# An inverse and a solve whose matmuls go over more columns than are used

## The chip, the cores and the metric

The kernel runs on one core of a Trainium2 chip. The metric is the device time of one execution in microseconds: 1938.36 us before the change, the median of three runs from 1925.35 to 1941.91.

## The reference, cut to what matters

One inference step of a two-layer recurrent decoder trunk, for a prompt of 528 tokens (16 meta tokens and 512) and 32 sample tokens (8 sequences of 4), width 1024. Layer 0 mixes with gated linear attention (GLA) and an RWKV-7 recurrence side by side; layer 1 mixes with gated DeltaNet (GDN). Each mixer is followed by a convolutional feed-forward part. The change touches what stands for the two recurrences. For GDN the reference has it openly, chunk by chunk:

```python
a_mat = jnp.where(strict, jnp.einsum('bhlk,bhmk->bhlm', ki, ki) * dec, 0.0) * bi[..., :, None] + eye
rhs = jnp.concatenate([vi * bi[..., None], ki * (bi * jnp.exp(gam))[..., None]], axis=-1)
sol = lax.linalg.triangular_solve(a_mat, rhs, left_side=True, lower=True, unit_diagonal=True)
```

RWKV-7 is a scan over tokens in the reference (`s = s * w + (s a) b + v k`); the kernel brings it into the same form, a unit triangular system for each tile of tokens.

## The kernel before, in words

**Tiles.** The 560 tokens stand in five tiles of 112, 112, 112, 96 and 128 (`TILES`; the last has 96 prompt and 32 sample tokens). A "row" count of 112, 96 or 128 below is the length L of such a tile. Heads are taken four at a time: RWKV has two groups of four heads, GDN too. So each of the two recurrences has 2 x 5 tiles, and for every one of them `prep` builds four triangular matrices, calls `tri_inverse` (L708 on) and then `tri_solve` (L769 on), and `step` carries the state on. `core(g)` (L1117 for RWKV, L1774 for GDN) calls `prep(i)` ahead of `step(i-1)`, so one tile's inverse stands beside the state step of the tile before.

**The inverse.** `tri_inverse` doubles block inverses in fp16: T starts as the transpose of the inverse of 2x2 blocks, W as that inverse itself. At level q, with blocks of b = 2, 4, ... 64 columns, four matmuls (one for each head) make `px` = a x T (L737), VectorE masks it into `X` (L738), four make `pt` (L747) and four `pw` (L753), and VectorE adds them to T (L758) and W (L765). Every second block of b columns holds what is new, so `px` and `pt` go over those columns alone (`up`, which is `upper(ap, b, L)`): 56, 48 or 64 of 112, and so on. `pw` goes over all L columns. `X` is set to zero by GpSimd (L734) before VectorE writes the new blocks. The last level (b = 64) has no `pt`. So an inverse has six `px`, five `pt` and six `pw`, each of four matmuls.

**The solve.** `tri_solve` works in fp32r with one refinement step: p0 = W r, p1 = (three terms with x0: identity, `ah`, `al`), p2 = W times the residual. `prod` (L777) issues, for each head i, one matmul a term over the `kd` right sides of that head (`kd` x `w` columns). For RWKV w is 64, for GDN 128; kd is 2, except in a group's first tile, where it is 1. So RWKV's matmuls have 128 columns (64 in the first tile) and GDN's 256 (128 in the first tile).

**What runs beside it, and the order.** While a group's tiles are worked on, a generator issues the projections of later work (`k.beside`, `k.tick`): matmuls at L148, three for each product because fp32 is split into high and low parts. RWKV's first group has them all the way, its second group has GLA's own loop (L1250 to L1330: `pr`, `pv`, `pa`, `po`, `pS`) beside it instead; GDN's groups have GDN's projections and gates, and the norm of the first group (L201, L217). The order of each engine's instructions is set when the program is built: the framework plans it from priorities and its own costs of instructions, and each engine then works strictly in that order.

Of the kernel before, what the change touches and what calls it, by code (L numbers as in the profile page):

```python
# [688 lines left out]
def upper(ap, b, L):  # L689

    m = pairs(b, L)
    if m == 1:
        return ap[..., 0:b]
    return ap[..., 0 : 2 * b * m].rearrange("... (k c) -> ... k c" if len(ap.shape) == 2 else "p n (k c) -> p n k c", c=2 * b)[..., 0:b]


def lower(ap, b, L):

    full = L // (2 * b)
    out = []  # L700
    if full:
        out.append(ap[:, :, 0 : full * 2 * b].rearrange("p n (k c) -> p n k c", c=2 * b)[:, :, :, b : 2 * b])
    if L - full * 2 * b > b:
        out.append(ap[:, :, full * 2 * b + b : L])
    return out


def tri_inverse(k, pool, pp, tag, lv, a, Wr, L, n):  # L708

    nc = k.nc
    two = lambda name: pool.tile([128, 2, n, 128], F16, tag="so" + tag, name=name, bufs=2)
    ps = lambda name: pp.tile([128, n, 128], F32, tag="mx" + tag, name=name)
    bc = lambda ap: ap.unsqueeze(1).to_broadcast([L, n] + list(ap.shape[1:]))
    ta, wx = two("ta"), two("wx")
    T, a16, W = ta[:, 0], ta[:, 1], wx[:, 0]
    Xs = [pool.tile([128, n, 128], F16, tag="X" + tag, name="X"), wx[:, 1]]
    nc.scalar.copy(a16[:L, :, :L], a[:L, :, :L])  # L720
    nc.vector.tensor_mul(W[:L, :, :L], a[:L, :, :L], bc(lv[:L, 0, :L]))
    nc.vector.tensor_add(W[:L, :, :L], W[:L, :, :L], bc(k.ident16[:L, :L]))
    p0 = ps("p0")
    for i in range(n):
        nc.tensor.matmul(p0[:L, i, :L], W[:L, i, :L], k.ident16[:L, :L], start=True, stop=True)
    nc.scalar.copy(T[:L, :, :L], p0[:L, :, :L])
    for q in range(1, 7):
        b = 1 << q
        if b >= L:
            break  # L730
        k.tick()
        up = lambda ap: upper(ap, b, L)
        X = Xs[q % 2]
        nc.gpsimd.memset(X, 0.0)  # L734
        px = ps("px")
        for i in range(n):
            nc.tensor.matmul(up(px[:L, i]), a16[:L, i, :L], up(T[:L, i]), start=True, stop=True)  # L737
        nc.vector.tensor_tensor(up(X[:L]), up(px[:L]), bc(up(lv[:L, q])), op=ALU.mult)  # L738
        last = 2 * b >= L
        k.tick()  # L740
        if not last:
            pt = ps("pt")
            ta = cfg("TA", 0) and (n == 4 or cfg("TB", 1))
            for i in range(n):
                if ta:
                    nc.tensor.matmul(up(pt[:L, i]), k.ident16[:L, :L], up(T[:L, i]), start=True, stop=False)
                nc.tensor.matmul(up(pt[:L, i]), W[:L, i, :L], up(X[:L, i]), start=not ta, stop=True)  # L747
        pw = ps("pw")
        wa = False and not last
        for i in range(n):  # L750
            if wa:
                nc.tensor.matmul(pw[:L, i, :L], k.ident16[:L, :L], W[:L, i, :L], start=True, stop=False)
            nc.tensor.matmul(pw[:L, i, :L], X[:L, i, :L], W[:L, i, :L], start=not wa, stop=True)  # L753
        if not last:
            if ta:
                nc.scalar.copy(up(T[:L]), up(pt[:L]))
            else:
                nc.vector.tensor_add(up(T[:L]), up(pt[:L]), up(T[:L]))  # L758
        else:
            nc.scalar.copy(Wr[:L, :, 0:b], W[:L, :, 0:b])  # L760
        for p, v, w in zip(*(lower(x[:L], b, L) for x in (pw, Wr if last else W, W))):
            if wa:
                nc.scalar.copy(v, p)
            else:
                nc.vector.tensor_add(v, p, w)  # L765
    return Wr


def tri_solve(k, pool, pp, tag, sub, W, ah, al, idr, R, L):  # L769


    nc = k.nc
    _, kd, n, w = R.shape
    m = min(n, 512 // (kd * w))
    tl = lambda name: pool.tile([128, kd, m, w], F32R, tag="so" + tag, name=name, bufs=2)

    def prod(name, terms):  # L777
        t = pp.tile([128, m, kd, w], F32, tag="mx" + tag, name=name)
        for i in range(m):
            for j, (a, x) in enumerate(terms):  # L780
                nc.tensor.matmul(t[:L, i], a(h0 + i), x[:L, :, i], start=(j == 0), stop=(j == len(terms) - 1))  # L781
        return t[:L].rearrange("p n k v -> p k n v")

    h = lambda a: lambda i: a[:L, i, :L]
    for h0 in range(0, n, m):
        r = R[:L, :, h0 : h0 + m]
        rr = tl("sol_r")
        nc.scalar.copy(rr[:L], r)
        p0 = prod("p0", [(h(W), rr)])
        k.tick()  # L790
        x0 = tl("sol_x")
        nc.scalar.copy(x0[:L], p0)
        p1 = prod("p1", [(lambda i: idr[:L, :L], x0), (h(ah), x0), (h(al), x0)])
        k.tick()
        rr2 = tl("sol_r")
        (nc.vector.tensor_sub if sub else nc.vector.tensor_add)(rr2[:L], r, p1)
        if cfg("RA", 0) and sub:
            p2 = prod("p2", [(lambda i: idr[:L, :L], x0), (h(W), rr2)])
            nc.scalar.copy(r, p2)
        else:  # L800
            p2 = prod("p2", [(h(W), rr2)])
            nc.vector.tensor_add(r, p2, x0.bitcast(F32)[:L])


class RWKV:
# [113 lines left out]
    def prep(self, prs, i):  # L919
# [38 lines left out]
        if ty and cfg("RS", 0) == 1:  # L958
            self.sr = self.read_states(prs)
        W = tri_inverse(k, self.pc, self.mx, par, self.lv, ma[:, 0], P("Wr", [128, 4, 128], F32R), L, 4)  # L960
        pv = bank([128, 4, 64], "pv")
        for h in range(4):
# [425 lines left out]
class GDN:  # L1388
# [195 lines left out]
    def prep(self, g, kq, i):  # L1584
# [56 lines left out]
        if ty and cfg("GS", 1):  # L1641
            sr = self.read_states(g, ks, Gr, R, bank)
        W = tri_inverse(k, self.p1, self.mx, par, self.lv, A, P("Wr", [128, 4, 128], F32R), L, 4)
        if ty and not cfg("GS", 1):
            sr = self.read_states(g, ks, Gr, R, bank)
# [251 lines left out]
def trunk(tc, a, o):  # L1897
# [7 lines left out]
    y=(128, KT, NT), shift=(128, KT, 9), gla_p=(2, 128, 128), gla_s=(2, 128, 8, 128), rwkv_p=(4, 128, 64),  # L1905
# [35 lines left out]
```

## Time and profile before

| | before |
| --- | --- |
| median of three runs | 1938.36 us (1925.35 to 1941.91) |
| profiled execution: time | 1941.04 us |
| profiled execution: span from first to last instruction | 1939.1 us |
| TensorE matmul busy | 1820.7 us, 94% |
| VectorE, ScalarE, GpSimd busy | 1169.9, 751.6, 437.9 us |
| mean granted TensorE clock | 0.949 of full speed |

In the rows, PE is TensorE's matmuls, DVE is VectorE, ACT ScalarE, POOL GpSimd. A matmul's form is written as rows of the moving operand * output rows, then rows x columns. Matmuls are pipelined, so a single one lasts some 0.2 to 0.4 us by its own, while the next starts much earlier; what a stream of them costs is seen from start to start. Where several equal ones follow each other, the timeline shows them as one row with a count, from the first start to the last end. PEclk is the granted TensorE clock: 1.00 is 2.4 GHz and 0.50 is 1.2 GHz. RWKV's groups lie at about 80 to 290 us and 260 to 480 us, GDN's at about 1100 to 1270 us and 1270 to 1420 us; the feed-forward parts lie behind each.

### The profile page before, as it was taken

The page shows a single profiled execution, that of the slowest core. Times are in us where ns is not written, and L with a number is a line of the kernel's source. Part 1 is how long each engine was busy: PE and PEld are TensorE (multiplying, and loading weights), DVE is VectorE, ACT ScalarE, POOL GpSimd, SP SyncE. Part 2 cuts the span into 40 slices and gives each one's busy share as a digit, 9 for nine tenths or more (in the row PEclk, how much of TensorE's full clock was granted, in tenths as well). Part 3 has the DMA queues.
Part 4 walks back from the last instruction along what each step waited for, and adds up shares of the span by engine and source line. Part 5 has one row for each costly group of instructions (what it writes and reads, how often), then busy time and mean ns, then how long its engine had stood idle before and what let it go on. Part 6 is the DMA issues. An engine that isn't in the chain of part 4 may idle for free.

```text
span 1939.1 us, 34294 instructions
## 1 busy us (share of the span) xinstructions
PE 1820.7 (94%) x13877; PEld 1694.1 (87%) x13877; DVE 1169.9 (60%) x2085; ACT 751.6 (39%) x1396; POOL 437.9 (23%) x705
## 2 busy tenths in 40 slices
PE   8998899899989999999979999899989999999996
PEld 8897788676889999999968997788679899999995
DVE  5766434446786535535776787687578653453466
ACT  6563323344353223213455454444244432232233
POOL 1323334212241000000141343332236200000001
PEclk9999999669899999999988999999789999999998
DMA  5110122301412222222322212412233122222231
GB/s 205 51 38 23 57 82 82 97 19 38 158 37 79 86 88 88 87 84 85 101 70 61 77 37 63 145 65 74 64 119 108 38 87 88 88 88 88 88 92 47
DMA packets 67358, 153.64 MB, mean 79 GB/s; under 512 B 15656, under 2 KB 26728, under 8 KB 67200
## 3 DMA queue, kind: packets, MB, share of 16 engines
q1 hardware_dynamic: 62784, 142.68, 23.9%
q10 hardware_dynamic: 3104, 4.15, 0.7%
q0 software_dynamic: 1312, 4.63, 0.6%
q8 instruction: 109, 1.79, 0.4%
q14 instruction: 49, 0.40, 0.1%
HBM read 136.72 MB, written 14.70 MB: 78 GB/s over the span
## 4 chain that ended last, share of the span: by engine, by line
PE 58%; DVE 9%; DMA 2%; issue 2%; ACT 2%; POOL 1%; POOLq 0%; SPq 0%; ACTq 0%; DVEq 0%
PE pd L148 13%; PE pg L148 13%; PE pu L148 13%; PE ph L148 7%; PE lead L148 2%; PE p L781 1%; DVE r L511 1%; DVE r L564 1%; DVE r L563 1%; PE psr L272 1%; PE pn L201 1%; PE pst L544 1%; PE pS L1701 1%; PE pw L753 1%; PE pm L1625 1%
## 5 line engine op out<-in xcount | busy, mean ns | idle before, releaser
L95 ACT CAST wh<-wraw 128x1024 fp32r<-128x1024 f32 x179 | 187.4, 1047 | 471.3 <-issue 163.2
L96 DVE TENSOR_TENSOR wl<-wraw,wh 128x1024 fp32r<-128x1024 f32 x158 | 193.9, 1227 | 205.9 <-ACT wh L95 205.9
L148 PE MATMUL ph<-xh,wh 128*128 128x280 f32 (+3 forms) x928 | 287.9, 311 | 16.1 <-ACT cp L1510 7.8
L148 PE MATMUL ph<-xh,wl 128*128 128x280 f32 (+3 forms) x928 | 285.8, 308 | 0.0
L148 PE MATMUL ph<-xl,wh 128*128 128x280 f32 (+3 forms) x928 | 285.7, 308 | 0.0
L148 PEld LDWEIGHTS ph<-xh,wh 128*128 128x128 f32 x928 | 181.1, 195 | 25.0 <-ACT cp L1510 8.0
L148 PE MATMUL pg<-xh,wl 128*128 128x264 f32 (+3 forms) x640 | 186.7, 292 | 0.0
L148 PE MATMUL pu<-xh,wl 128*128 128x264 f32 (+3 forms) x640 | 186.7, 292 | 0.0
L148 PE MATMUL pg<-xh,wh 128*128 128x264 f32 (+3 forms) x640 | 186.0, 291 | 0.0
L148 PE MATMUL pu<-xh,wh 128*128 128x264 f32 (+3 forms) x640 | 185.9, 291 | 0.0
L148 PE MATMUL pu<-xl,wh 128*128 128x264 f32 (+3 forms) x640 | 185.7, 290 | 0.0
L148 PE MATMUL pg<-xl,wh 128*128 128x264 f32 (+3 forms) x640 | 185.7, 290 | 0.0
L148 PEld LDWEIGHTS ph<-xh,wl 128*128 128x128 f32 x928 | 180.9, 195 | 5.2 <-issue 3.7
L148 PEld LDWEIGHTS ph<-xl,wh 128*128 128x128 f32 x928 | 181.1, 195 | 4.5 <-issue 3.1
L380 POOL COPY cn<-gp 128x2 f32<-128x2 f32 x44 | 31.3, 712 | 573.2 <-ACT gp L378 573.2
L148 PE MATMUL pd<-hl,wh 128*128 128x280 f32 (+1 forms) x512 | 148.8, 291 | 0.1
L148 PE MATMUL pd<-hh,wl 128*128 128x280 f32 (+1 forms) x512 | 148.7, 291 | 0.0
L148 PE MATMUL pd<-hh,wh 128*128 128x280 f32 (+1 forms) x512 | 147.8, 290 | 0.0
L148 PEld LDWEIGHTS pg<-xh,wh 128*128 128x128 f32 x640 | 120.9, 189 | 0.0
L148 PEld LDWEIGHTS pu<-xh,wh 128*128 128x128 f32 x640 | 120.9, 189 | 0.0
L148 PEld LDWEIGHTS pg<-xl,wh 128*128 128x128 f32 x640 | 120.7, 189 | 0.0
L148 PEld LDWEIGHTS pu<-xl,wh 128*128 128x128 f32 x640 | 120.7, 189 | 0.0
(552 smaller groups left out, 4637.7 us busy)
## 6 DMA issues: line engine op xcount, KB each, us to landing
wraw<-in_w_up SPq DMA_DIRECT2D x88, 512.0 KB, 3.5
wraw<-in_w_down SPq DMA_DIRECT2D x32, 512.0 KB, 3.6
wraw<-in_w_c SPq DMA_DIRECT2D x32, 512.0 KB, 3.7
wraw<-in_w_ab SPq DMA_DIRECT2D x26, 512.0 KB, 3.6
wraw<-in_w_down SPq DMA_DIRECT2D x16, 384.0 KB, 3.7
wraw<-in_w_oab SPq DMA_DIRECT2D x8, 512.0 KB, 4.0
sb<-in_s_gdn SPq DMA_DIRECT2D x16, 256.0 KB, 2.8
so<-in_s_gdn SPq DMA_DIRECT2D x16, 256.0 KB, 3.3
```

The lines of the kernel that those rows point to most:

```text
L95: self.nc.scalar.copy(hi, src)
L96: (eng or self.nc.vector).tensor_sub(lo, src, hi.bitcast(F32))
L148: self.nc.tensor.matmul(ps[:, :m], a[:, i, :], x[:, i, c : c + m], start=(i == 0 and n == 0), stop=(i == k - 1 and n == 2))
L201: last = mm(ps[32 * j : 32 * j + 32, :m], w[:, 0:32], x(j, slice(c, c + m)), start=(i == 0), stop=(i == len(terms) - 1))
L272: k.nc.tensor.matmul(ps, z[:, 64 * b : 64 * b + 64], s[:, b % 4], start=(b == 0), stop=(b == 7))
L380: nc.gpsimd.tensor_copy(cn[:, f, 0, :], gp[:, P:G])
L511: st(y, y, 1.0 if i < 4 else self.alpha, cb, op0=ALU.mult, op1=ALU.subtract)
L544: mm(ps[:, i, 0:w], k.o1024, y, start=(n == 0), stop=(n == len(xs) - 1))
L563: nc.vector.tensor_mul(t, t, rs)
L564: nc.vector.tensor_sub(t, t, mean)
L753: nc.tensor.matmul(pw[:L, i, :L], X[:L, i, :L], W[:L, i, :L], start=not wa, stop=True)
L781: nc.tensor.matmul(t[:L, i], a(h0 + i), x[:L, :, i], start=(j == 0), stop=(j == len(terms) - 1))
```

## The change

`px` and `pt` go over all L columns instead of `up`'s; what VectorE takes from them stays the same (`up(px)`, `up(pt)`), so the added columns are not used. In `tri_solve` a head's matmul goes over its own columns and over those of the heads that follow, until 256 columns are reached or the heads end: 128 columns become 256, 256, 256 and 128 for the four heads, 64 become 256, 192, 128 and 64, and 256 stay. The next head's matmuls then write its columns anew.

```diff
         for i in range(n):
-            nc.tensor.matmul(up(px[:L, i]), a16[:L, i, :L], up(T[:L, i]), start=True, stop=True)
+            nc.tensor.matmul(px[:L, i, :L], a16[:L, i, :L], T[:L, i, :L], start=True, stop=True)
...
-                nc.tensor.matmul(up(pt[:L, i]), W[:L, i, :L], up(X[:L, i]), start=not ta, stop=True)
+                nc.tensor.matmul(pt[:L, i, :L], W[:L, i, :L], X[:L, i, :L], start=not ta, stop=True)
...
     def prod(name, terms):
         t = pp.tile([128, m, kd, w], F32, tag="mx" + tag, name=name)
         for i in range(m):
+            e = min(m, i + max(1, 256 // (kd * w)))
             for j, (a, x) in enumerate(terms):
-                nc.tensor.matmul(t[:L, i], a(h0 + i), x[:L, :, i], start=(j == 0), stop=(j == len(terms) - 1))
+                y = x[:L, :, i:e].rearrange("p k n v -> p n k v")
+                nc.tensor.matmul(t[:L, i:e], a(h0 + i), y, start=(j == 0), stop=(j == len(terms) - 1))
```

No instruction is added or taken away, but the planner sets another order in both stretches with inverses. In the changed program the lines of the inverse stand one further down (L738, L748, L754) and those behind `prod` three (L784 for L781).

The first place is on TensorE in RWKV's second group, at the end of the second tile's solve and the start of the third tile's inverse (`p` of L781 is the solve's product, `p` of L725 the inverse's first transpose, `pv`, `pk` and `pa` are GLA's). Before:

```order
L781 MATMUL p_4212<-sol_x,al 112x128
L1269 MATMUL pv<-cst,vf 112x128 x4
L1274 MATMUL pk<-cst,ra_3179 112x128 x2
L781 MATMUL p_4228<-sol_r,Wr 112x128 x4
L725 LDWEIGHTS wx
L725 MATMUL p_4338<-ident_180,wx 112x112
```

and in the changed program:

```order
L726 LDWEIGHTS wx
L726 MATMUL p_4338<-ident_180,wx 112x112
L1277 MATMUL pk<-cst,ra_3179 112x128
L784 MATMUL p_4228<-sol_r,Wr 112x256 x3
L784 MATMUL p_4228<-sol_r,Wr 112x128
L1300 MATMUL pa_3666<-kb,qt_3571 32x112
L738 LDWEIGHTS ta
L738 MATMUL px<-ta 112x112
```

The solve's last product, now three matmuls of 256 columns and one of 128, stands behind the next inverse's transposes and not ahead of them, and the first `px` follows it sooner.

The second place is on TensorE in GDN's second group, in the first level of the last tile's inverse (128 rows; `pS` and `py` belong to the state step, `pn` to the norm of the first group, `pg` to the end of the solve before). Before, from the last `px` of the level to its first `pt`:

```order
L737 MATMUL px<-ta 128x32x2
L1701 MATMUL pS<-U,kt 128x128 x2
L1706 MATMUL py<-Gr,S 128x96
L1709 MATMUL py<-E,U 128x96
L747 LDWEIGHTS wx
L747 MATMUL pt<-wx 128x32x2
```

and in the changed program:

```order
L738 MATMUL px<-ta 128x128
L201 MATMUL pn<-kq,cst 32x280
L201 MATMUL pn<-kq,eo 32x280
L201 MATMUL pn<-kq,cst 32x280
L201 MATMUL pn<-kq,eo 32x280
L201 MATMUL pn<-kq,cst 32x280
L201 MATMUL pn<-kq,eo 32x280
L201 MATMUL pn<-kq,cst 32x280
L1656 MATMUL pg<-cst,R 128x96 x2
L201 MATMUL pn<-kq,eo 32x432
L748 LDWEIGHTS wx
L748 MATMUL pt<-wx 128x128
```

Norm matmuls that stood ahead of this inverse, in the tile before, now stand between its first two products, and the state step's matmuls come later in it.

## Rows read from the trace of the kernel before

**Rows 1.** The page: busy time of the engines, granted clock in 40 slices.
```profile
PE 1820.7 (94%) x13877; PEld 1694.1 (87%) x13877; DVE 1169.9 (60%) x2085; ACT 751.6 (39%) x1396; POOL 437.9 (23%) x705
PEclk9999999669899999999988999999789999999998
```

**Rows 2.** Stretches (from:to us): length, then busy us of each engine (instructions), clock.
```profile
core 0: us, PE busy (x) PEld busy (x) DVE busy (x) ACT busy (x) POOL busy (x), PEclk, DMA share, GB/s
368.00:418.00 50.00, 50.00 (x294) 40.09 (x293) 16.85 (x60) 13.53 (x43) 7.53 (x11) 0.50 0.06 11
419.00:448.00 29.00, 27.13 (x259) 20.53 (x258) 18.77 (x56) 12.92 (x32) 5.89 (x15) 1.00 0.10 29
448.00:476.00 28.00, 26.00 (x232) 18.39 (x229) 17.57 (x41) 14.77 (x34) 8.21 (x13) 1.00 0.16 41
1364.00:1388.00 24.00, 22.24 (x135) 15.80 (x135) 11.81 (x31) 7.69 (x12) 4.50 (x8) 0.58 0.19 57
1187.00:1203.00 16.00, 13.60 (x151) 11.75 (x151) 13.80 (x31) 9.77 (x16) 6.48 (x10) 1.00 0.22 68
```

**Rows 3.** Timeline of PE, start and length in us: idle times before 361 us.
```profile
349.85 1.01 PE L781 MATMUL p<-sol_r,Wr 112*112 112x128 f32 x4 [2.28 <-ACT sol_r L788]
...
357.15 1.07 PE L1269 MATMUL pv<-cst,vf 128*112 128x128 f32 x4 [3.11 <-DMA vf<-z_v]
...
361.23 1.01 PE L781 MATMUL p<-sol_r,Wr 112*112 112x128 f32 x4 [2.59 <-DVE sol_r L796]
```

**Rows 4.** Timeline of PE: first and last product of two inverses.
```profile
362.04 0.57 PE L725 MATMUL p<-ident,wx 112*112 112x112 f16 x4
...
393.42 0.62 PE L753 MATMUL pw<-wx,X 112*112 112x112 f16 x4
...
419.34 0.34 PE L725 MATMUL p<-ident,wx 96*96 96x96 f16 x4
...
434.16 0.38 PE L753 MATMUL pw<-wx,X 96*96 96x96 f16 x4
```

**Rows 5.** Waits (total us, times, longest) in 361 to 418, then 419 to 448.
```profile
DVE ta L758 <- PE pt L747: 10.3, 4, 7.4
...
DVE ta L758 <- PE pt L747: 2.4, 3, 0.9
```

**Rows 6.** Timeline of PE at full clock: narrow fours and `pw`.
```profile
148.39 0.34 PE L737 MATMUL px<-ta 112*112 112x56 f16 x4
...
150.80 0.39 PE L753 MATMUL pw<-wx 112*112 112x112 f16 x4
...
456.60 0.28 PE L747 MATMUL pt<-wx 128*128 128x64 f16 x4
456.72 0.39 PE L753 MATMUL pw<-wx 128*128 128x128 f16 x4
```

**Rows 7.** Timeline of PE: neighbours in p1 at 128 and at 256 columns.
```profile
168.16 0.26 PE L781 MATMUL p<-sol_x,ah 112*112 112x128 f32 x1
168.26 0.26 PE L781 MATMUL p<-sol_x,al 112*112 112x128 f32 x1
...
1155.48 0.28 PE L781 MATMUL p<-sol_x,ah 112*112 112x256 f32 x1
1155.60 0.28 PE L781 MATMUL p<-sol_x,al 112*112 112x256 f32 x1
```

**Rows 8.** Timeline of PE at half clock: fours of one level, next `px`.
```profile
363.86 0.53 PE L737 MATMUL px<-ta 112*112 112x56 f16 x4
...
366.30 0.60 PE L753 MATMUL pw<-wx 112*112 112x112 f16 x4
...
367.87 0.53 PE L737 MATMUL px<-ta 112*112 112x56 f16 x4
```

**Rows 9.** Timeline of PE: the inverse that starts in the second slow stretch.
```profile
1363.88 0.61 PE L725 MATMUL p<-ident,wx 128*128 128x128 f16 x4
...
1382.94 0.61 PE L753 MATMUL pw<-wx,X 128*128 128x128 f16 x4 [0.59 <-DVE X L738]
```

## The prediction

> **What bounds the kernel now.** I read the page first: TensorE is busy in 94% of the span, and its slices of granted clock are near full except about slices 7 to 8 [rows 1]. So a change to matmuls is a change to the busiest engine, and a stretch at the lower clock stands inside the part that the change touches. Next I cut the span into stretches. The inverses and solves lie in 80 to 480 us and 1100 to 1440 us. Between 368 and 418 us the granted clock was 0.50 of 2.4 GHz, so 1.2 GHz, TensorE was busy for 50.00 of 50.00 us, and it got through 294 matmuls, 5.9 in a microsecond. In the 29 us from 419 and the 28 us from 448 the clock was 1.00, and it got through 259 and 232, that is 8.9 and 8.3 in a microsecond, of the same two loops (the second head group's steps and the gated attention beside them) [rows 2]. The other engines do less than half their time in 368 to 418, so this stretch is paced by a half-speed TensorE, not by a chain elsewhere.
>
> What the engine did before the clock fell stands in the timeline: it sat idle for 2.28 us until ScalarE's `sol_r`, a little later for 3.11 us until a DMA, and for 2.59 us until VectorE's `sol_r` [rows 3]. The change does not shorten these waits, so I expect the fall again. From 361 us the engine is fed without a pause, and yet the level stays at 1.2 GHz for 57 us more. One inverse started at 362.04 and its last product at 393.42, 31.4 us; the next took from 419.34 to 434.16, 14.8 us [rows 4]. The waits agree: in 361 to 418 us VectorE stood 10.3 us for `pt` in four waits, in 419 to 448 us 2.4 us in three [rows 5].
>
> **The change part by part.** *Wider `px` and `pt`.* They come in fours: 20 inverses of six `px` and five `pt` products, so 480 and 400 matmuls. The third product of a level, `pw`, has always gone over all columns, so it is the row for the new width. A four of 56 columns on 112 rows took 0.34 us from its first start to its last end, a four of `pw` at 112 columns 0.39; on 128 rows, 0.28 against 0.39 [rows 6]. That is 0.05 us more in each of 16 inverses x 11 fours, 8.8 us (the 96-row ones, four of the 16, taken at the same price), and 0.11 us more in 4 x 11 fours, 4.8 us. Together 13.6 us.
>
> *Wider solves.* A solve has five products of four matmuls (p0, three terms of p1, p2). Three of each four go from 128 to 256 columns in the eight RWKV solves with two sides and in GDN's two first tiles; in RWKV's two first tiles only two of four grow by enough to matter; the other eight GDN solves had 256 already and do not change. Starts at 128 columns stand 0.10 us apart, at 256 columns 0.12 us [rows 7]: twice the columns for 0.02 us, since the narrow ones were not paced by their columns. 150 matmuls in ten solves and 20 in two, by 0.02 us, are 3.4 us.
>
> So the columns cost 17.0 us if all of it lies on the path, and 0 if it is all beside other work. What can hide it: filler projections stand ready on TensorE in most of both stretches, and each level waits on VectorE between its products. But the added time lies inside a chain (`px`, X, `pt`, T, next `px`), and TensorE has little idle time for it. Three pairs of inverses overlap, so there it is paid once for two. I take a little more than half, 9 us, and keep 0 and 17.
>
> Here a rule weighs against the change more than the rows do. In rows 6 the narrow four on 112 rows takes longer (0.34 us) than the one on 128 rows (0.28), though it has fewer columns, 56 against 64: its columns do not pace it, and widening them costs little. The Trainium skill (TensorE: Matmul & The Clock Gate, Back-to-back issue gap) gives N / 2.4 + 2.5 ns for a matmul, by which, as an estimate, 56 more columns are 23 ns and 64 are 27 ns each, 0.09 and 0.11 us a four. The trace does not agree on 112 rows and agrees on 128. By that rule the two products would cost 21 us, not 13.6, and with half of it on the path the sum would end some 4 us later.
>
> *Clock.* At 1.2 GHz the fours took 0.53 us at 56 columns and 0.60 at `pw`'s 112 [rows 8]: twice the columns in nearly the same time, so the engine streams more of the time there. I take it that the level comes back where the stream has few pauses: the engine idled before the fall, and what is left of pauses behind 361 us lies inside narrow matmuls. No row shows how much is enough, so A below keeps a fair chance. A level lasts about 4 us there, from one `px` at 363.86 to the next at 367.87 [rows 8], and eight matmuls with 56 columns more, at 1.2 GHz, stream for 0.37 us more in it. I expect the rise after the first level or two, at about 368 us instead of 418. What it is worth: 294 matmuls at 8.6 in a microsecond (the mean of 8.9 and 8.3) take 34.2 us instead of 50.0, 16 us less. Bounds: 0 if the clock does not rise earlier; 25 if all 50 us run at twice the speed. The same rule of the clock stands in the Trainium skill (same page, The HAM clock gate): activity releases the throttle. The trace agrees in direction only.
>
> *The second slow stretch.* In 1364 to 1388 us the mean clock was 0.58, with 135 matmuls in 24 us; the same tile of the other head group did 151 in 16 us at 1.00 [rows 2], so all of it at full clock would be 14.3 us, 10 less. This inverse has 128 rows, where each of its 11 fours costs 0.11 us more or double that at the low clock, and the order there is new. I take 3 us for a somewhat earlier rise, bounds 0 and 10.
>
> *Order.* The planner moves rows on all engines inside both stretches. The two places shown with the change are the ones my terms rest on. At the first, the next inverse's first transposes stand before the last product of the solve ahead of them, which fills one of the waits before 361 us; at the second, norm matmuls of 280 columns stand between the products of an inverse, which keeps the engine streaming but lengthens that inverse. By my count of the order, up to 35 fewer projection matmuls stand ahead of an inverse in the second stretch; they come later, not more often. I cost the order at 0, with 10 us either way as its bound, the size of one such slow stretch.
>
> **Sum.** The profiled execution has 1941.0 us, of which 1939.1 is span. 1941.0 + 9 (columns) - 16 (clock in 368 to 418) - 3 (clock in 1364 to 1388) = 1931.0. The median of the three times is 1938.4 and they lie between 1925.4 and 1941.9, so the profile is as long as the longest of them, and the 7 us that I go below the median are within what they differ by.
>
> **Rivals.** *A, ends slower:* the wider columns do not bring the clock back earlier. For it: the level held for 57 us of fed engine [rows 2, 4], and the added columns are only 0.37 us in a level of 4 us. Against it: the pauses that end the streaming are those of narrow fours. Then 9 to 17 us are paid for nothing: 1950 to 1958. It decides once the clock's gain is below the columns' cost, so if the stretch from 368 us on is still at 0.50 for more than some 25 us.
>
> *B, more gain:* once up, the clock stays up through both stretches, and the columns hide behind waits: 1941.0 + 4 - 25 - 4 = 1916, or down to 1910 with the whole of 10 us in the second stretch. For it: in 419 to 476 us it stayed at 1.00 [rows 2] with the same loops and no fillers. Against it: VectorE and ScalarE have their own chains, so twice the clock is not twice the pace.
>
> *C, the order:* the clock does as I say, but the new order delays a solve or a norm on the path by 10 to 25 us: 1941 to 1956. For it: hundreds of rows moved. Against it: the inverses start after nearly the same number of matmuls as before.
>
> **How the numbers follow.** My forecast (earlier rise, about half of the columns paid) has a chance of 0.47 and its own range of 1921 to 1940; A 0.25, B 0.17, C 0.11. A measurement of this kernel can tell about 1% from no change, so faster is below 1919.0 and slower above 1957.7. Faster takes most of B and a little of the forecast's low end: 0.18. Slower takes the end of A and of C: 0.08. The rest, 0.74, is the same. The range of 1910 to 1952 leaves out the upper end of A and of C and little below.
>
> **What would show each step.** Fours of `px` and `pt` at 0.39 us on 112 and 128 rows, and 0.12 us between solve matmuls, show the prices. The row of the stretch that answers 368 to 418 us shows the clock: 1.00 for most of it and an inverse of about 16 us there are my case; 0.50 throughout is A. A clock at 1.00 and the same 57 us from one inverse to the next would show that TensorE did not pace that stretch, and the prediction wrong in its main term. In the second stretch I look for the time from 1364 us to the end of that inverse, 20 us now [rows 9]. If the warm inverses lengthen by much more than 0.6 us (11 fours by 0.05) on 112 rows, or 1.2 us on 128, the columns' price or the order was mis-sized.

## The result: 1915 us, with 67 us less at 1.2 GHz in the profile

The changed kernel took 1915.15 us, the median of four runs (1914.23 to 1919.0), beside 1936.87 us for before (1925.35 to 1941.91): a ratio of 0.990 with a 95% interval of 0.985 to 0.995. Two later comparisons of the same kernel, among the experiments below, gave 0.993 (0.989 to 0.997) and 0.991 (0.987 to 0.995). So the gain is real and lies between half a per cent and one and a half, about the size of what one comparison can tell from no change. Here and below, runs that took over 1.5% longer than the fastest of their kernel are left out (nine of the 75 listed one by one for before in the experiments, one of e6's and one of e9's). The time is inside the range on record (1910 to 1952) and 16 us below the 1931.0 forecast.

The profiled execution took 1915.0 us, its span 1913.2 us. The page's lines that answer [rows 1]:

```profile
PE 1798.6 (94%) x13877; PEld 1677.1 (88%) x13877; DVE 1164.0 (61%) x2085; ACT 752.0 (39%) x1396; POOL 442.8 (23%) x705
PEclk9999999689989999999989999899989999999998
```

TensorE is as full as before; where before had two slices at 6 in a row (7 and 8), there is one. The stretches that answer [rows 2], from windows of the changed kernel (columns as there). The first row lies from one inverse's start to the next one's; the six after it cut the time from 343.4 us at each turn of the clock; the last two are the second slow stretch and, for comparison, its sister in the first head group:

```profile
354.60:400.40 45.80, 45.80 (x378) 36.26 (x377) 23.20 (x86) 20.33 (x63) 8.51 (x12) 0.71 0.11 23
343.40:363.90 20.50, 13.84 (x98) 11.23 (x99) 11.11 (x28) 10.03 (x31) 6.30 (x13) 0.50 0.45 144
363.90:370.70 6.80, 6.80 (x71) 6.08 (x71) 4.71 (x22) 1.97 (x7) 1.60 (x3) 1.00 0.01 2
370.70:380.90 10.20, 10.20 (x88) 8.65 (x86) 4.49 (x15) 4.99 (x15) 2.51 (x6) 0.50 0.10 20
380.90:391.20 10.30, 10.30 (x77) 8.58 (x77) 3.36 (x12) 3.99 (x11) 2.11 (x2) 1.00 0.01 2
391.20:398.10 6.90, 6.90 (x54) 4.27 (x53) 4.14 (x16) 3.13 (x11) 0.98 (x3) 0.51 0.34 68
398.10:415.10 17.00, 16.27 (x144) 11.79 (x143) 9.04 (x30) 8.25 (x21) 2.91 (x5) 1.00 0.08 23
...
1335.80:1359.80 24.00, 22.23 (x181) 14.07 (x181) 16.30 (x37) 12.38 (x22) 7.41 (x12) 1.00 0.37 114
1170.00:1186.00 16.00, 15.45 (x147) 13.01 (x145) 12.67 (x26) 9.51 (x15) 5.77 (x12) 1.00 0.30 101
```

The level came back at 363.9 us, 54 us earlier than before's 418.1 us, but it did not stay: it fell again at 370.7, at 391.2 and at 415.1 us. From the start of the third tile's inverse to that of the fourth took 45.8 us and not 57.3 (362.0 to 419.3, [rows 4]). The second slow stretch ran at 1.00 throughout. The timeline of TensorE (columns as in [rows 3]) has the idle times around the first fall, a block that ends shortly before each of the two next, the first and the last matmuls of two inverses, and the start of the one between them:

```profile
343.84 1.09 PE L784 MATMUL p<-sol_r,Wr 112*112 112x256 f32 x4 [2.02 <-ACT sol_r L791]
...
351.15 0.43 PE L1272 MATMUL pv<-cst,vf 128*112 128x128 f32 x1 [6.22 <-DMA vf<-z_v]
...
354.64 0.58 PE L726 MATMUL p<-ident,wx 112*112 112x112 f16 x4
...
368.20 1.86 PE L1259 MATMUL pr<-qm,sb 128*128 128x8 f32 x16
...
380.12 0.58 PE L754 MATMUL pw<-wx,X 112*112 112x112 f16 x4
...
387.44 1.95 PE L1259 MATMUL pr<-qm,sb 128*128 128x8 f32 x16
...
400.43 0.34 PE L726 MATMUL p<-ident,wx 96*96 96x96 f16 x4
...
1335.80 0.40 PE L726 MATMUL p<-ident,wx 128*128 128x128 f16 x4
...
1354.68 0.40 PE L754 MATMUL pw<-wx,X 128*128 128x128 f16 x4
```

The wait for `sol_r` in which the first fall came is still there (2.02 us, up to 343.84 us, where [rows 3] had 2.28), so the fall itself stayed, as forecast; the wait of 6.22 us for a DMA lies behind the fall, as do the 3.11 and the 2.59 us of [rows 3]. The two next falls come 0.6 and 1.8 us behind the end of a block of `pr`, GLA's read, whose matmuls have 8 columns (each of them leaves two records in the trace). In the same stretch VectorE now stood 5.3 us for `pt`, against 10.3 in [rows 5]; its row of the waits from 354.6 to 400.4 us:

```profile
DVE ta L759 <- PE pt L748: 5.3, 3, 2.9
```

### The profile page after: what moved, and what is told of

Its sections match the earlier page's. It is cut to its first block, busy times and chain, and to the rows that moved or that the text cites. A ratio compares the mean times of both kernels' runs of the same rounds, so it can differ in the third digit from the quotient of the medians.

```text
span 1913.2 us, 34292 instructions
## 1 busy us (share of the span) xinstructions
PE 1798.6 (94%) x13877; PEld 1677.1 (88%) x13877; DVE 1164.0 (61%) x2085; ACT 752.0 (39%) x1396; POOL 442.8 (23%) x705
## 4 chain that ended last, share of the span: by engine, by line
PE 75%; DVE 10%; ACT 4%; DMA 4%; issue 3%; POOL 3%; SPq 0%; POOLq 0%; ACTq 0%; DVEq 0%
PE ph L148 14%; PE pd L148 12%; PE pg L148 12%; PE pu L148 12%; PE lead L148 2%; PE p L784 2%; PE pm L950 2%; PE px L738 1%; PE pw L754 1%; PE psr L272 1%; PE pt L748 1%; DVE r L511 1%; DVE vl L96 1%; PE pn L201 1%; PE pst L544 1%
```

## The experiments

Eleven runs. In nine of them the program is built twice: once as the program whose order is wanted, and once as the one that runs, in which every engine is pinned to the first one's order, row by row. So columns and order can be had apart:

```diff
+    order = [(i.name, str(i.engine)) for i in build(arrays, {...}).all_instructions()]   # whose order
+    nc = build(arrays, {...}, order)                                                     # what is wide
...
+            for name, engine in order:
+                if name in here:
+                    if engine in last:
+                        tc.add_manual_dep(here[name], last[engine], NoSync, reason="order")
+                    last[engine] = name
```

Theory 1 at the start: the columns bring the clock back, and the gain is theirs. Theory 2: the planner's new order is the gain, and columns only cost.

**How the runs are read.** The kernels here differ by little over a per cent at most, and before by itself ranges from 1915 to 1950 us in the runs used. What tells its runs apart is the clock. Each run lists its span and mean granted clock; with two levels, the time that it spent at 1.2 GHz is 2 x (1 - clock) x span (for the profile of before 198 us; the sum of its stretches is 199). Over the 168 runs that the comparisons rest on, one line fits: time = a constant of the kernel + 0.364 us (0.347 to 0.381) for each microsecond at 1.2 GHz, with 1.9 us of scatter. In before's 66 runs alone the slope is 0.362 and the correlation 0.97. So each kernel has two numbers: its microseconds at 1.2 GHz, and its constant against before's, the time at equal clock:

```
                              runs  mean us  us at 1.2 GHz  at equal clock, against before
before                          66   1931.9      179.3        0
changed kernel, three calls     22   1917.5      138.7       +0.4 (-0.8 to +1.5)
e1 all wide, old order          10   1928.7      155.3       +5.5 (+4.2 to +6.8)
e2 narrow, new order            10   1926.8      183.3       -6.6 (-7.8 to -5.4)
e3 px, pt wide, old order       10   1925.5      155.5       +2.2 (+0.9 to +3.5)
e4 solves wide, old order       10   1934.4      179.8       +2.3 (+1.1 to +3.5)
e5 second groups, old order     10   1926.2      160.1       +1.3 ( 0.0 to +2.6)
e6 first groups, old order       9   1933.4      177.7       +2.1 (+0.8 to +3.4)
e7, e10 changed + wide read     10   1910.4      118.7       +0.5 (-1.1 to +2.2)
e9 before + wide read           11   1925.4      155.3       +2.1 (+0.8 to +3.4)
```

One run's us at 1.2 GHz are known to about 2 us (the clock is listed to a thousandth), and before's mean of them was 188, 171 and 177 in the three calls. Against before in its own call the mean of an edited kernel is known to 11 to 15 us (95%), so smaller differences there are not read. The last column takes a microsecond at 1.2 GHz to cost the same wherever it stands, and its intervals hold under that alone: had e1's 24 us less cost 0.32 or 0.43 each, prices met below, its +5.5 would be +4.4 or +7.1.

**e1: wide columns, old order.** `{"inv": True, "sol": True}` in the order of `{}`. The only difference to before is the shape of 1060 matmuls.

```diff
+    order = [... build(arrays, {}) ...]
+    nc = build(arrays, {"inv": True, "sol": True}, order)
```

> All products wide as in the changed kernel, but every engine's instructions in the order of the kernel before, row for row. Theory 1 (the wide columns bring the clock back earlier): 12 to 26 us faster than before (the whole gain of the change was 21.7 us between medians), with the 1.2 GHz stretch of 68 us behind 350 us shortened to under 45 us. Theory 2 (the planner's new order brings the gain and the columns cost): 5 to 17 us slower than before, the stretch at 1.2 GHz as long as before.

Measured: 1929.84 us median, ratio 0.997 (0.994 to 1.000). Neither theory's number. The line shows why: against before in its call e1 has 32 us less at 1.2 GHz, worth 11.8 us, and the columns cost 5.5; together -6.3, and the means have -6.0. One number of theory 1 was missed: its profile has 51 us at 1.2 GHz between 340 and 430 us (349.5 to 366.6 and 376.8 to 410.9), where under 45 were expected.

**e2: narrow columns, new order.**

```diff
+    order = [... build(arrays, {"inv": True, "sol": True}) ...]
+    nc = build(arrays, {}, order)
```

> All products narrow as before, but every engine's instructions in the order of the changed kernel. Theory 1 (columns and clock): within 6 us of before. Theory 2 (the order): 20 to 35 us faster than before, since the order's gain is there and no columns are paid.

Measured: 1927.34 us median, ratio 0.996 (0.993 to 0.998), 8.2 us below before's median in the call. Theory 1 is wrong in saying that the order does nothing, theory 2 in the size. The time at 1.2 GHz is that of before, and the gain stands at equal clock: the order is worth 6.6 us by itself.

**e3 and e4: one part alone, old order.**

```diff
+    nc = build(arrays, {"inv": True}, order)   # e3: px and pt
+    nc = build(arrays, {"sol": True}, order)   # e4: the solves
```

> Only px and pt wide, in the order of before. Theory 1, if the inverse carries it (it adds 13.6 us of columns, the solves 3.4): 10 to 22 us faster than before, nearly what all wide gives in that order. If the solves carry it: within 6 us of before. Theory 2: 4 to 14 us slower.

> Only the solves wide, in the order of before. Theory 1 with the inverse carrying it: within 5 us of before. If the solves carry it: 10 to 22 us faster. Theory 2: 0 to 4 us slower.

Measured: e3 1924.57 us, ratio 0.995 (0.991 to 0.998), so -11.0 by the medians (-9.2 by the means), the near end of theory 1's range; e4 1931.47 us, 0.999 (0.996 to 1.002), which doesn't tell the two apart. `px` and `pt` have all of the clock's gain (155.5 us at 1.2 GHz, as with all wide), the solves none that can be told. At equal clock they cost 2.2 and 2.3 us, together 4.5 beside e1's 5.5.

These four made **theory 3**: time is the columns' cost, plus the order's gain, plus 0.364 us for each microsecond at 1.2 GHz; columns change the last. Its rival, **theory 4**: the level falls and rises by chance of timing, and any shift of the program gives another pattern.

**e5 and e6: wide in the second or in the first head groups alone, old order.** Before's long stretches at 1.2 GHz lie in the second groups.

```diff
+    nc = build(arrays, {"inv": ("rwkv1", "gdn1"), "sol": ("rwkv1", "gdn1")}, order)   # e5
+    nc = build(arrays, {"inv": ("rwkv0", "gdn0"), "sol": ("rwkv0", "gdn0")}, order)   # e6
```

> px, pt and solves are wide in the second groups of RWKV and GDN alone (255 to 480 and 1270 to 1420 us), every engine in the order of before. Theory 3, made after the first four runs: time is a cost of the added columns at equal clock (5.9 us for all of them) plus 0.37 us for every microsecond at 1.2 GHz, and wider products shorten the stretches at 1.2 GHz where these are long, which is in the second groups. Then this kernel has nearly the whole of the clock's gain (us at 1.2 GHz down by 30 to 45 from before's 195, against 39 where all is wide) and half of the cost: time -7 to -13 us. Theory 4: the level falls and rises by chance of timing, and any shift of the program gives another pattern; then the gain does not stand where the long stretches are: us at 1.2 GHz down by 10 to 30, time -8 to +1.

> px, pt and solves are wide in the first groups alone (80 to 290 and 1100 to 1270 us), every engine in the order of before. In the first groups before was at 1.2 GHz for some 20 us only, in short pieces. Theory 3: half of the columns' cost at equal clock, +2 to +4, little change of the clock (-10 to +5 us at 1.2 GHz), so time -1 to +5. Theory 4 (timing by chance): us at 1.2 GHz down by 10 to 30 as in the other half, time -8 to +1.

Measured: e5 1926.09 us, ratio 0.999 (0.995 to 1.002), e6 1935.56 us, 1.001 (0.997 to 1.005). The sides are as theory 3 has them: against all runs of before e5 is 19 us lower at 1.2 GHz and e6 within 2. The size is not: against before in the same call e5 is only 10.5 us lower, where 30 to 45 were expected, and by time alone neither can be told from before. By its size e5 alone is as theory 4 has it. This pair doesn't decide; the wide read does.

**e7: the changed kernel, with the read widened.** GLA's read has 8 columns a matmul, and its 32 records end within 2 us ahead of the falls at 370.7 and 391.2 us. If narrow matmuls let the level fall, wide ones at this one place should hold it. Every engine keeps the changed kernel's order. The edit, with the run's switch for it written out:

```diff
-            pr = bank([128, 8, 2, 4], "pr")
+            pr = bank([128, 31, 2, 4], "pr")
             for n in range(8):
-                mm(pr[:, n], d["sb"][:, n], qm[:, :, 4 * n : 4 * n + 4], start=True, stop=True)
+                q = qm[:, :, 4 * n : 4 * n + 4].unsqueeze(1).to_broadcast([128, 24, 2, 4])
+                mm(pr[:, n : n + 24], d["sb"][:, n], q, start=True, stop=True)
...
-            nc.scalar.copy(os[:, 2 * p : 2 * p + 2].rearrange("p h (b c) -> p b h c", c=4), pr)
+            nc.scalar.copy(os[:, 2 * p : 2 * p + 2].rearrange("p h (b c) -> p b h c", c=4), pr[:, :8])
```

> The changed kernel, every engine in its order, and in GLA's read (pr, 2 x 8 fp32 matmuls of 8 columns, 368 and 387 us in the changed kernel's profile) every matmul goes over 24 copies of its 8 columns, 192, the first 8 of which are used. After both blocks of pr the granted clock of the changed kernel fell (at 370.7 and 391.2 us). A pr record takes 109 ns from start to start at 8 columns, and one of 128 columns (psr) takes the same, so the columns should cost 0 to 1 us. Theory 3 (columns keep the level up): no fall behind either pr; 10 to 17 us less at 1.2 GHz than the changed kernel beside it, time -3 to -7 us against it. Theory 4 (the level falls for the idle times and the changes of the order, or by chance, and not for narrow matmuls): the falls at 370 and 391 us remain, time within 2 us of it, or above by up to 1.

**e8: the changed kernel beside it**, without an edit.

> The changed kernel itself, on the chip of the three others and beside its runs of before. Both theories: its ratio to before is that of the first comparison, 0.985 to 0.995, so 10 to 29 us faster; by the line through the runs (0.37 us for each microsecond at 1.2 GHz) its us at 1.2 GHz are 50 to 65 below before's and its time at equal clock is within 3 us of before's. It is the base for the wide read.

Measured: e8 1920.17 us, ratio 0.993 (0.989 to 0.997), as expected, but with 27 us less at 1.2 GHz than before in its call, not the 50 to 65 expected; e7 1911.56 us, 0.988 (0.982 to 0.995). By the means e7 is 8.8 us (4.0 to 13.5) below e8, with 21 us less at 1.2 GHz: theory 3, and a little more than its number. In e7's profile no fall follows either block of `pr`; the next one comes at 398.9 us, 11 us behind the second block's end.

**e9: the same edit on before**, narrow columns, old order. The diff is e7's.

> The kernel before, every engine in its order, px, pt and solves narrow, and only GLA's read (pr, 16 fp32 matmuls) at 192 columns each, of which 8 are used. In the profile of before both blocks of pr lie inside the 68 us at 1.2 GHz (378.7 and some 405 us), where a record of pr took 213 ns with 8 columns. Theory 3 (the level comes back where the columns stream): the stretch after 350 us ends earlier in most runs, 10 to 35 us less at 1.2 GHz than before, time -4 to -13 us, with nothing lost at equal clock (within 2). Theory 4 (pr does not matter; in the wide read on the changed kernel the clock's pattern moved by chance): us at 1.2 GHz within 6 of before's, time within 2 us.

Measured: 1925.1 us, ratio 0.997 (0.994 to 1.000), 6.1 us below before by the medians, and 22 us less (7 to 36) at 1.2 GHz than before in its call. So sixteen matmuls of GLA, which have no part in the inverse, do to the clock much of what 880 matmuls of the inverse do in e3 (32 us less in its call). At equal clock the edit costs 2.1 us, just above the 2 allowed for. Its profile alone doesn't show how: the level is back at 366.1 us, but so it is, with the narrow read, in e4 and e6 (366.9 and 365.1).

**e10 and e11: the wide read and the changed kernel again**, with more runs; the kernels are those of e7 and e8.

> The wide read on the changed kernel once more, with more runs, beside the changed kernel on one chip. Theory 3: as in the first look, 10 to 20 us less at 1.2 GHz than the changed kernel beside it and 4 to 9 us faster than that. Theory 4: within 3 us of the changed kernel; the four runs of the first look were lucky ones.

> The changed kernel again, beside the two others. Both theories: 10 to 20 us faster than before in the same call, and time at equal clock within 2 us of before's.

Measured: e10 1909.85 us, ratio 0.989 (0.985 to 0.993), e11 1915.02 us, 0.991 (0.987 to 0.995). By the means e10 is 5.4 us (1.9 to 9.0) below e11, with 18 us less at 1.2 GHz. Theory 4 falls as to the mean: the read's edit took 21, 22 and 18 us at 1.2 GHz away in three comparisons, while e2, e4 and e6, which shift the program too, stayed within 8 us of before in their calls. For the single run chance stays: before's have from 134 to 226 us at 1.2 GHz, and no run here says why. In the profiles, 340 to 430 us has 38 and 31 us at 1.2 GHz with the wide read and 41 to 44 in the changed kernel's three, about half of the gain; where the rest lies isn't shown. And the changed kernel with the wide read is the fastest of this study, below both kernels. TensorE's rows of e10: the two blocks of `pr`, and windows of the stretch at 1.2 GHz, of the first block and of the second:

```profile
369.83 2.79 PE L1275 MATMUL pr<-qm,sb 128*128 128x192 f32 x16
...
385.56 2.88 PE L1275 MATMUL pr<-qm,sb 128*128 128x192 f32 x16
```

```profile
343.50:367.40 23.90, 17.08 (x116) 14.44 (x117) 12.80 (x37) 11.12 (x35) 6.77 (x14) 0.50 0.38 121
367.40:380.00 12.60, 12.51 (x145) 10.86 (x144) 7.34 (x30) 5.66 (x19) 3.98 (x7) 1.00 0.08 18
380.00:411.00 31.00, 29.95 (x262) 22.65 (x261) 14.96 (x51) 14.77 (x39) 5.69 (x7) 1.00 0.11 28
```

From 367.4 to 411 us the level stays up through both blocks. Over all profiles of this study, 14 blocks of `pr` with 8 columns began at 2.4 GHz, and behind ten of them the level fell within 2 us of the block's end (in one, just before its end); of five wide blocks that began at 2.4 GHz none had one so soon (the next came after 11 us or more). In the new order it was seven of seven narrow blocks beside none of four wide ones. All four narrow blocks without a fall are the first block in the old order (e3 to e6), so the block alone does not decide: what else stands around it counts too.

## Why the prediction was right or wrong

The forecast's side and its range held; its sum came 16 us too high, and each of its three kinds of term has a part in that. That it came so near is in part luck: its largest term rested on a stretch that stands in none of the other twelve profiles.

**Columns (+9 on record, measured +5.5; 4.2 to 6.8).** The prices were read rightly, as the shares of one four: `px` and `pt` now take what `pw` takes, and the solve's matmuls at 256 columns stand 0.11 to 0.12 us apart, as [rows 6, 7] had it. Timeline rows of the changed kernel:

```profile
149.92 0.36 PE L738 MATMUL px<-ta 112*112 112x112 f16 x4
...
385.91 0.28 PE L784 MATMUL p<-sol_x,al 112*112 112x256 f32 x1
386.03 0.28 PE L784 MATMUL p<-sol_x,idr 112*112 112x256 f32 x1
...
434.62 0.39 PE L738 MATMUL px<-ta 128*128 128x128 f16 x4
...
436.35 0.40 PE L748 MATMUL pt<-wx 128*128 128x128 f16 x4
```

What failed is how much of it lies on the path. Before and e1 have the same order, so inverses that run at 2.4 GHz in both give the price directly (from the first transposes to the start of the last `pw` matmul):

```
start in before, rows        before     e1     longer by
147.4, 112                   16.68    16.70      0.02
174.9,  96                   15.03    15.13      0.10
419.3,  96                   14.98    15.09      0.11
448.0, 128                   15.68    16.70      1.02
1138.1, 112                  14.86    14.87      0.01
1159.1,  96                  17.28    17.27     -0.01
1187.5, 128                  13.42    14.16      0.74
```

On 112 and 96 rows the forecast was 0.6 us an inverse, and it is 0.1 or nothing: what the wider fours take is hidden there (four more such inverses, left out of the table, differ by -0.1 to 0.1). On 128 rows it was 1.2, and it is 0.7 and 1.0. The 1.0 repeats: that inverse takes 15.68 us in before, e4, e6 and e9, where its columns are narrow, and 16.70 in e1, e3 and e5. The timelines show it: the first transposes and the last product of the inverse from 448 us in before, and of the same one in e1:

```profile
447.96 0.39 PE L725 MATMUL p<-ident,wx 128*128 128x128 f16 x4
...
463.47 0.39 PE L753 MATMUL pw<-wx,X 128*128 128x128 f16 x4
```

```profile
440.98 0.39 PE L733 MATMUL p<-ident,wx 128*128 128x128 f16 x4
...
457.51 0.39 PE L767 MATMUL pw<-wx,X 128*128 128x128 f16 x4
```

The rule that the prediction weighed against the rows (the Trainium skill, TensorE: Matmul & The Clock Gate, Back-to-back issue gap; the section gives it for a matmul by itself and says that it counts too little for a small one in a stream with weight loads) would have had an inverse on 112 rows longer by 11 x 0.09 = 1.0 us, as an estimate. The trace does not agree on 112 rows (0.0 to 0.1), and on 128 rows it agrees in size.

**Clock in 368 to 418 us (-16 on record).** The rise came where it was forecast (363.9 for some 368), the idle time ahead of the fall stayed, and the price was nearly right: 16 us for 50 us at 1.2 GHz is 0.32 a microsecond, and the runs have 0.364. Two readings behind this term were wrong, though. Of the three idle times of [rows 3] only the first lies ahead of the fall, at 349.8 us in before; the other two stand at 1.2 GHz already:

```profile
340.00:350.00 10.00, 7.50 (x61) 5.87 (x60) 6.28 (x21) 4.24 (x11) 5.31 (x8) 0.99 0.47 140
350.00:361.00 11.00, 4.86 (x22) 3.98 (x22) 6.42 (x10) 5.44 (x15) 4.60 (x11) 0.50 0.81 261
```

And that wider columns brought the level back is not shown. It came back between 363 and 370 us in all twelve other profiles, also where `px` and `pt` of this stretch are narrow: e2 (366.4), e4 (366.9), e6 (365.1) and e9 (366.1). Windows of e4, then of e6:

```profile
346.50:366.90 20.40, 12.45 (x91) 10.73 (x91) 11.04 (x27) 10.65 (x31) 6.73 (x14) 0.50 0.46 149
366.90:384.00 17.10, 16.89 (x180) 13.96 (x180) 10.67 (x44) 8.79 (x30) 4.50 (x8) 1.00 0.06 13
...
344.70:365.10 20.40, 12.55 (x93) 10.65 (x93) 11.34 (x29) 11.19 (x34) 6.69 (x14) 0.50 0.47 149
365.10:389.00 23.90, 23.69 (x232) 19.52 (x231) 11.82 (x48) 9.72 (x32) 5.15 (x9) 1.00 0.05 10
```

So the 68 us of before's profile are one execution's. Over ten runs each, wider `px` and `pt` do lower the time at 1.2 GHz (e1, e3), but between 340 and 430 us the profiles don't tell the two apart: 68, 41 and 27 us in before, e4 and e6, and 51, 27 and 41 in e1, e3 and e5. Where in the program these columns act stays open. The step that failed by its size is that the level, once back, stays. Between 340 and 430 us the profile of before has 68 us at 1.2 GHz and the changed kernel's 44, so 24 us went and not some 50; that is 9 us by the line, and 57.3 to 45.8 us from one inverse to the next. The inverse in it did not come to 16 us, it took 25.8 (from 354.64 to the start of its last matmul). That narrow matmuls of another loop stand in this stretch could be seen in the timeline of before, and I gave them no thought:

```profile
378.73 3.58 PE L1256 MATMUL pr<-qm,sb 128*128 128x8 f32 x16
...
406.09 3.58 PE L1256 MATMUL pr<-qm,sb 128*128 128x8 f32 x16
```


**Second stretch (-3 on record).** The clock's part was too small, was put down to the wrong cause, and is not what the inverse gained. The level stayed up there with the new order and not for the columns: in the six profiles with that order 1300 to 1400 us has 0 to 3 us at 1.2 GHz, in the seven with the old one 10 to 27, and e2, whose columns are narrow, has none. Its window of that inverse:

```profile
1344.10:1362.40 18.30, 16.88 (x153) 9.96 (x154) 12.76 (x30) 10.59 (x21) 7.10 (x10) 1.00 0.39 121
```

All of it was at 1.00 in the changed kernel, and yet that inverse took 19.1 us, about as long as in before (19.4), where most of it was at 1.2 GHz [rows 9]. The old order shows both halves: in e3 the same inverse, with 4 us at 1.2 GHz, took 15.8 us, and in e2 and the changed kernel, in the new order and at full clock, 18.3 and 19.1. So the new order, which has norm matmuls between its products, took back what the clock gave. They were not lost: from 1335.8 us the changed kernel got through 181 matmuls in 24 us, where before did 135 from 1364 us on [rows 2], and that work need not be done elsewhere. It looks like the sign that the prediction named for a stretch which TensorE's level doesn't pace, but by e3's 15.8 us the level does pace this inverse in the old order.

**Order (0 on record, measured -6.6; -7.8 to -5.4).** This is the largest miss in kind: I had it as a bound of 10 either way, with a rival for delay alone. Where e2 gains can only be read from one pair of profiles. Its 2,000th matmul, at the end of RWKV's first group, starts 3.7 us earlier at equal clock; by the end of RWKV that is back to about 1; by 1340 us, in GDN, it is 7.6, and 8.1 at the end. From 1070 to 1340 us TensorE sat idle for 13.4 us in e2 where before had 16.1, so not all of it is filled waits. Two inverses of GDN are 3 us shorter in that order (the one from 1159 us 14.4 and not 17.3) and a third is 1 us shorter, while two are 1 and 2 us longer. Which moved rows do it was not tried.

**The sum.** For the two profiles: columns +5.5, order -6.6, and 67.4 us less at 1.2 GHz (198.8 to 131.4) by 0.364, -24.5; together -25.6, and 1941.0 to 1915.0 is -26.0. Part of the 67 is the choice of the profiles: 20 of them stand at 470 to 570 and 970 to 1075 us, largely outside the change, and vary from run to run; before's profile was one of its longer runs. Over all runs it is 41 us, so 5.5 - 6.6 - 14.8 = -15.9, beside a measured -14.4.

**The rivals.** A did not come by its sign: the stretch from 368 us was not at 0.50; but its ground, that the columns do not bring the level back in that stretch, is not refuted. B came in its second half (the columns largely hidden on 112 rows, the second stretch at 1.00, though by the order) and not in its first. C had the order's sign wrong. Most of the chances stood on a change within 1%; the three comparisons have 1.0, 0.7 and 0.9%, so the result lies at the edge of that.

## What to carry to other kernels

Where a kernel's runs differ by more than a change is worth, put each run's time against its time at 1.2 GHz first: columns, order and clock then come apart, and a change of 5 us can be read among runs 35 us apart. A narrow matmul that its columns don't pace can be widened at little cost, and what that bought here stands not in its own row but in the time at 1.2 GHz. After predicting that a level comes back, look through the stretch for the next narrow block that could send it down again. And before resting a term on one slow stretch, look at a second profile of the same program: the one here lasted until 418 us in one profile of thirteen.

## What the runs showed of the hardware

- The level can fall on an engine for which the profile shows no idle time. Ahead of the fall at 370.7 us TensorE was busy for 6.80 of 6.80 us; in it stood 8 matmuls of 8 columns (16 records in 1.86 us), which ended 0.6 us before the fall. The Trainium skill speaks of idle gaps there (TensorE: Matmul & The Clock Gate, HAM oscillation — how this bites in real kernels); the trace agrees for the fall at 343.4 us, which came inside an idle time of 2.02 us, and shows another way for the two after it.
- A microsecond at 1.2 GHz cost 0.364 us (0.347 to 0.381) of this kernel's time, not half. In part of those stretches TensorE waits, as from 343.4 us on (busy for 13.84 of 20.50 us), which can be the reason. In one inverse with hardly any idle time (TensorE busy for 31.70 of 31.70 us in before, 20.82 of 21.03 in e3) it was more: 31.7 us with 32 at 1.2 GHz in before, 21.0 with 7 in e3, so 0.43.
- 192 columns in fp32 are not free: a wide block of `pr` took 2.79 us where 8 columns took 1.86, so 1.9 us for both blocks, about what e9 lost at equal clock (2.1) and twice what I expected at most. On the changed kernel no such loss shows (+0.5 with the wide read, +0.4 without).
